# A two-layer encoder trunk in fp32r: another mixer, with scores on row halves, two heads' probabilities side by side, another order of products, and an output projection fed with normalised blocks

## The chip, the core and the metric

The kernel runs on one core of one Trainium2 chip. That core has TensorE (PE, with weight loads shown apart as PEld), VectorE (DVE), ScalarE (ACT), GpSimd (POOL) and SyncE (SP), which here only issues DMAs. The metric is device time in microseconds of one execution, lower is better. The chip has a multiplier array of 128 rows; a matmul multiplies a stationary tile (loaded first) with a moving tile and adds into one of eight PSUM banks of 128 x 512 floats.

## The reference, cut to what matters

The trunk has two layers on x of 256 tokens x 1024 channels. Each layer is a half-step SwiGLU, the mixer, a second half-step SwiGLU, and a gated per-layer input; a final norm follows. Only the mixer is changed:

```python
u = rmsnorm(x, g_mix[i]) @ w_in[i]
q, k, v, hy = jnp.split(u, [NA_WIDTH, 2 * NA_WIDTH, 3 * NA_WIDTH], axis=-1)
hs = (B, L, NA_HEADS, NA_HEAD_DIM)          # 8 heads of 64
y_na = neighbourhood_attention(q.reshape(hs), k.reshape(hs), v.reshape(hs), na_rpb[i])
hy = short_conv(hy, w_sc[i], b_sc[i])        # width 3 over the tokens
x0, x1, hv = jnp.split(hy, 3, axis=-1)
filt = implicit_filter(...)                  # independent of x
y_hy = x0 * long_conv(hv * x1, filt, hy_bias[i])
y = jnp.concatenate([_rms(y_na), _rms(y_hy)], axis=-1) * g_out[i]
x = x + y @ w_out[i]
```

Attention is a masked softmax over the 256 tokens for each of the 8 heads; `_rms` divides each token's 512 channels by their root mean square, once for the attention half (NA) and once for the convolution half (HY).

## The kernel before

Channels lie on the 128 partitions and the 256 tokens along the free axis, so x is eight tiles of 128 x 256. Every product is made with operands split into a high and a low fp32r part: `mm3` (lines 169 to 173) issues high x high, high x low and low x high. Weights stream from HBM in pieces of 16 tiles; ACT casts the high part (line 285) and DVE or, for every third half piece in the mixer, POOL subtracts to get the low part (line 288). Six half pieces are held ready.

The order of the program comes from generators ("fibers"). The main program issues PE work; after every three units of it (a unit is an `mm3` on 256 columns) `tick` advances every live fiber by one step, the newest first. When PE work needs a fiber's result, `finish` runs `tick` until that fiber is done, without any PE work in between. PE and ACT run in the order in which the program recorded their instructions; DVE, POOL and SP stand in the order that a scheduler gave them when the program was built. Each queue is served strictly in its order.

The mixer (lines 662 to 1000) first makes the values of all heads, then follows the table `ORDER` (line 58), whose letters mean: `q` j, queries and keys of head pair j; `g` j, the two convolution inputs that are multiplied to u[j] (POOL, line 854); `x`, the outer gate x0; `s` j, the scores of pair j, followed by a softmax fiber (DVE bias and maximum, ACT exponential, DVE reciprocal, ACT rescale, line 779); `t` j, transposes of the probabilities (line 786) and their split in high and low; `p` j, probabilities times values; `u`, transposes of u; `f` 0 and 1, the forward transform of u, followed by `spectral` fibers (DVE products with the filter's spectrum, lines 900 and 901, POOL sums, line 906, ACT cast, line 910, DVE low part, line 912) that leave `yf`; `i` 0 to 3, the backward transform, which needs all four `yf`; `a` 0 to 7, the output projection's half for NA.

Three choices of the old code matter below. In `QK.go` the queries of the two heads of a pair are written into a zeroed 128-row tile, one head's rows at a time, so that each head's scores are a full-height matmul with half of its rows zero. In `attend` each head's values stand in zero-padded columns, so both heads add into one 128 x 256 result. In `head_norm` the blocks are scaled by the gain only; the projection starts on them at once, and the result of each projection is multiplied by the token's 1/rms afterwards (`add`, lines 942 and 943). The 1/rms comes from class `Rstd`: two small PE matmuls on the summed squares (line 418), a chain of small DVE instructions (lines 426 to 435) with two on ACT (line 436), and two PE matmuls with `ones` that spread it over the partitions (lines 442 and 443); `rest` counts the ticks between these steps.

Of the kernel before, what the change touches and what calls it, by code (L numbers as in the profile page):

```python
# [18 lines left out]
P = 128  # L19
T = 256  # L20
# [37 lines left out]
ORDER = "g0 q0 g1 s0 q1 g2 t0 s1 g3 q2 t1 p0 u0 q3 f0 s2 f1 p1 s3 t2 x0 x1 t3 i0 p2 p3 i1 i2 i3 a0 a1 a2 a3 a4 a5 a6 a7"  # L58
MIXER = [(t[0], int(t[1])) for t in ORDER.split()]

# [20 lines left out]
def hybrid_trunk(ctx: ExitStack, tc: tile.TileContext, w, xT, pT, rpb, small, wf, zT, dft, idft, decay, out):  # L81
# [322 lines left out]
    class Rstd:  # L404
# [6 lines left out]
        def go(self, parts, n, behind, at):  # L411
# [32 lines left out]
            S.copy(self.dst, ps)  # L444
# [222 lines left out]
    def mixer(i):  # L667
# [25 lines left out]
        vh = [[t2(F32R, "vh") for _ in range(2)] for _ in range(2)]  # L693
        vl = [[t2(F32R, "vl") for _ in range(2)] for _ in range(2)]

        def values():
            for tt in range(2):
                for pp in range(2):
                    G.memset(f(vh[tt][pp]), 0.0)
                    G.memset(f(vl[tt][pp]), 0.0)  # L700
            yield from rs.wait()
            for tt in range(2):
                vf = t2()
                V.tensor_scalar(vf, vps[tt], rs.r[:, tt : tt + 1], None, op0=ALU.mult)
                yield
                for pp in range(2):
                    src = vf[:, pp * 256 : (pp + 1) * 256].rearrange("p (a b c) -> p a b c", a=2, b=2)
                    hv, lv = v2(vh[tt][pp]), v2(vl[tt][pp])
                    for par in range(2):
                        cs = slice(par * 192, par * 192 + 64)  # L710
                        S.copy(hv[:, :, cs], src[:, :, par])
                    yield
                    for par in range(2):
                        cs = slice(par * 192, par * 192 + 64)
                        V.tensor_sub(lv[:, :, cs], src[:, :, par], f(hv[:, :, cs]))

        class QK:


            def __init__(self, b):  # L720
                self.kh, self.kl = t1(F32R), t1(F32R)
                self.qh, self.ql = t2(F32R), t2(F32R)
                self.fb = spawn(self.go(b))

            def go(self, b):
                G.memset(f(self.qh), 0.0)
                G.memset(f(self.ql), 0.0)
# [5 lines left out]
                where = [  # L733
                    (slice(64 * par, 64 * par + 64), slice(T * par, T * par + T)) for par in range(2)
                ]
                S.copy(self.kh, q[:, T:])
                for r, c in where:
                    S.copy(self.qh[r, c], q[r, :T])
                yield
                V.tensor_sub(self.kl, q[:, T:], f(self.kh))  # L740
                for r, c in where:
                    V.tensor_sub(self.ql[r, c], q[r, :T], f(self.qh[r, c]))

        class Head:
# [7 lines left out]
            def scores(self, st):  # L752
                st.fb.finish()
                b = bank()
                for tt in range(2):
                    qs = slice(T * self.par + tt * P, T * self.par + (tt + 1) * P)
                    mm3(b[:, tt * T : (tt + 1) * T], st.qh[:, qs], st.ql[:, qs], st.kh, st.kl, True, True)
                self.e = t2()
                self.fb = spawn(self.softmax(b), True)
# [21 lines left out]
            def turn(self):  # L781
                self.fb.finish()
                b = bank()
                for kt in range(2):
                    for tt in range(2):
                        PE.transpose(
                            b[:, kt * T + tt * P : kt * T + (tt + 1) * P],
                            self.e[:, tt * T + kt * P : tt * T + (kt + 1) * P],
# [471 lines left out]
```

## Time and profile before

| what | value |
|---|---|
| median of three runs | 1099.89 us (1099.7 to 1102.32) |
| the profiled execution | 1098.94 us, of which the span is 1097.2 us |
| mean granted TensorE clock | 0.994 |
| busy share of the span | PE 97%, DVE 83%, ACT 59%, POOL 24% |
| mixer of layer 1, of layer 2 | about 206.5 to 331 us, about 750 to 866 us of the span |

A row of the timeline gives the start in us, the busy time in us, engine, line, operation, written tile and read tiles, shape and how often; in brackets stands the idle time of that engine just before and the instruction that ended it. Instructions of one engine overlap in their records (a 256-column matmul lasts 0.28 us and the next starts 0.12 us later), so what one costs in a full queue is the distance from start to start.

### The profile page before, as it was taken

To read this page: it belongs to the slowest core of one execution; us is meant where nothing else is said; L and a number is where in the kernel's file an instruction comes from. 1 tells how busy PE (TensorE), PEld (TensorE's weight loads), DVE (VectorE), ACT (ScalarE), POOL (GpSimd) and SP (SyncE) were. 2 spreads that over 40 slices of the span, in tenths; PEclk is the share of its full clock that TensorE was granted. 3 is DMA by queue.
4 is the path that set the end of the run, shared out by engine and by line. 5 is a ranking of instruction groups with operands and counts; after the bars stand their busy time and mean duration, and the time that the engine had idled before them with its cause. 6 is when DMAs were issued, how large, how long until landed. Compare 5 with 4: busy or idle time off the path is not lost.

```text
span 1097.2 us, 18014 instructions
## 1 busy us (share of the span) xinstructions
PE 1066.1 (97%) x6716; PEld 964.1 (88%) x6716; DVE 912.0 (83%) x1552; ACT 649.2 (59%) x1182; POOL 266.1 (24%) x270
## 2 busy tenths in 40 slices
PE   7989999999998999999999999999999999999995
PEld 6878888899997888888988888889989888888895
DVE  4999987798999988856789999787899998886565
ACT  7566565367746766554666665544856476665444
POOL 3211120534363211100112113025442721110101
PEclk9989999999999999999999999999999999999998
DMA  8556545554425555555465654554622465554621
GB/s 318 199 202 227 192 163 183 177 180 163 154 78 201 196 192 193 188 192 177 169 211 184 231 192 158 188 177 168 194 78 90 151 220 202 192 192 159 208 94 39
DMA packets 32983, 194.07 MB, mean 177 GB/s; under 512 B 3584, under 2 KB 6528, under 8 KB 10880
## 3 DMA queue, kind: packets, MB, share of 16 engines
q1 hardware_dynamic: 32896, 192.92, 51.4%
q8 instruction: 53, 0.87, 0.3%
q14 instruction: 34, 0.28, 0.1%
HBM read 191.86 MB, written 1.05 MB: 176 GB/s over the span
## 4 chain that ended last, share of the span: by engine, by line
PE 79%; DVE 13%; ACT 4%; issue 3%; DMA 0%; POOL 0%; SPq 0%; DVEq 0%; ACTq 0%; POOLq 0%
PE ps L191 41%; PE ps L200 21%; PE ps L171 5%; PE ps L172 5%; PE ps L170 5%; DVE wl L288 3%; ACT wh L285 1%; DVE s L839 1%; DVE rt L399 1%; DVE x L943 1%; DVE s L942 1%; ACT t L779 1%; DVE xg L370 1%; ACT t L772 0%; DVE y L808 0%
## 5 line engine op out<-in xcount | busy, mean ns | idle before, releaser
L288 DVE TENSOR_TENSOR wl<-raw,wh 128x1024 fp32r<-128x1024 f32 (+1 forms) x328 | 405.3, 1258 | 103.2 <-PE ps L200 61.3
L285 ACT CAST wh<-raw 128x1024 fp32r<-128x1024 f32 (+1 forms) x350 | 362.4, 1042 | 157.0 <-PE ps L191 86.1
L191 PE MATMUL ps<-xg,wh 128*128 128x512 f32 x1408 | 347.3, 396 | 12.9 <-DVE xg L1091 6.7
L191 PEld LDWEIGHTS ps<-xg,wh 128*128 128x128 f32 x1408 | 260.0, 191 | 64.7 <-DVE xg L370 8.1
L200 PEld LDWEIGHTS ps<-xg,wl 128*128 128x128 f32 x1408 | 182.1, 191 | 7.7
L200 PE MATMUL ps<-xg,wl 128*128 128x256 f32 x1408 | 184.2, 283 | 0.0
L191 PE MATMUL ps<-act,wh 128*128 128x512 f32 x704 | 173.0, 391 | 0.0
L490 POOL TENSOR_TENSOR gu<-gu,rb 128x256 f32<-128x256 f32 x88 | 69.6, 796 | 394.4 <-DVE gu L208 326.3
L191 PEld LDWEIGHTS ps<-act,wh 128*128 128x128 f32 x704 | 128.3, 189 | 23.9
L356 POOL TENSOR_TENSOR acc<-acc,q 128x256 f32<-128x256 f32 x62 | 55.9, 902 | 295.0 <-ACT q L353 293.8
L170 PE MATMUL ps<-xg,wh 128*128 128x256 f32 x448 | 127.5, 285 | 0.0
L171 PE MATMUL ps<-xg,wh 128*128 128x256 f32 x448 | 126.7, 283 | 0.0
L172 PE MATMUL ps<-xg,wl 128*128 128x256 f32 x448 | 126.7, 283 | 0.0
L200 PEld LDWEIGHTS ps<-act,wl 128*128 128x128 f32 x704 | 92.9, 191 | 5.1
L200 PE MATMUL ps<-act,wl 128*128 128x256 f32 x704 | 94.4, 282 | 0.0
L171 PEld LDWEIGHTS ps<-xg,wh 128*128 128x128 f32 x448 | 85.9, 192 | 0.1
L170 PEld LDWEIGHTS ps<-xg,wh 128*128 128x128 f32 x448 | 85.9, 192 | 0.1
L172 PEld LDWEIGHTS ps<-xg,wl 128*128 128x128 f32 x448 | 85.9, 192 | 0.0
L205 ACT COPY gu<-ps 128x256 f32<-128x256 f32 x176 | 56.2, 374 | 33.1 <-PE ps L200 32.7
L288 POOL TENSOR_TENSOR wl<-raw,wh 128x1024 fp32r<-128x1024 f32 x22 | 56.1, 2550 | 64.0 <-ACT wh L285 51.2
L208 DVE TENSOR_TENSOR gu<-gu,ps 128x256 f32<-128x256 f32 x176 | 66.3, 413 | 0.0
L368 ACT ACTIVATE xg<-x,sm 128x256 fp32r<-128x256 f32 x56 | 28.2, 508 | 59.3 <-DVE x L527 39.9
(196 smaller groups left out, 1386.9 us busy)
## 6 DMA issues: line engine op xcount, KB each, us to landing
raw<-in_w SPq DMA_DIRECT2D x172, 1024.0 KB, 5.0
bias<-in_rpb SPq DMA_DIRECT2D x16, 256.0 KB, 2.9
raw<-in_w SPq DMA_DIRECT2D x4, 256.0 KB, 4.4
x<-in_xT SPq DMA_DIRECT2D x8, 128.0 KB, 5.0
raw<-in_w SPq DMA_DIRECT2D x2, 512.0 KB, 5.5
t<-in_wf SPq DMA_DIRECT2D x4, 256.0 KB, 5.6
dec<-in_decay SPq DMA_DIRECT2D x4, 256.0 KB, 6.3
out<-o SPq DMA_DIRECT2D x4, 256.0 KB, 2.5
```

Source lines behind the costliest of these rows:

```text
L170: PE.matmul(o, lh, rh, start=start, stop=False)
L171: PE.matmul(o, lh, rl, start=False, stop=False)
L172: PE.matmul(o, ll, rh, start=False, stop=stop)
L191: PE.matmul(b, lh, r, start=start, stop=False)
L200: PE.matmul(o, ll, rh, start=False, stop=stop)
L205: S.copy(dst, b[:, T:])
L208: V.tensor_add(dst, dst, b[:, :T])
L285: S.copy(h[:, a : a + k], src)
L288: e.tensor_sub(l[:, a : a + k], src, f(h[:, a : a + k]))
L356: G.tensor_add(self.ac, self.ac, q)
L368: S.activation(hl[:, :T], x[c], AF.Copy, scale=g)
L490: G.tensor_mul(u, u, rb)
```

## The change

The diff touches the mixer only (all line numbers after it are one or more off: `mm3` is lines 170 to 174 there):

- `QK`: queries and keys stay together in one 128 x 512 tile, split by one ACT cast and one DVE subtraction; the zeroed tiles are gone. `scores`: each head uses its own 64 rows of the array, and the matmuls of the two heads alternate, into two banks.
- `turn`: the two heads' transposed probabilities of one half of the keys share a bank. `attend`: one matmul on 512 columns serves both heads; two ACT copies take each head's 64 rows out of the bank, and the square follows on a later tick. Values need no padding.
- `Rstd` with `dst` True leaves 1/rms in its PSUM bank. `normed` and the new `head_norm` wait for it, multiply each block by gain and 1/rms (DVE), cast (ACT) and subtract (DVE); only then is a block ready for the projection. `add` is one DVE addition from PSUM to x. The NA half of the projection is issued after the four backward products, the HY half after it.
- `ORDER` is new; "g1+s0" puts the scores between the two products of g1. The weights are laid out in HBM in the new order.

```diff
-ORDER = "g0 q0 g1 s0 q1 g2 t0 s1 g3 q2 t1 p0 u0 q3 f0 s2 f1 p1 s3 t2 x0 x1 t3 i0 p2 p3 i1 i2 i3 a0 a1 a2 a3 a4 a5 a6 a7"
+ORDER = "q0 g0 q1 g1+s0 q2 g2+s1 t0 q3 p0 g3+s2 t1 x0+s3 u0 p1 t2 f0 t3 f1 p2 p3 x1 i0 i1 i2 i3"
...
-            S.copy(self.dst, ps)
+            if self.dst is True:
+                self.dst = ps
+            else:
+                S.copy(self.dst, ps)
...
+                S.activation(vh[tt], vps[tt], AF.Copy, scale=r)
+                yield
+                V.scalar_tensor_tensor(vl[tt], vps[tt], r, f(vh[tt]), op0=ALU.mult, op1=ALU.subtract)
...
+                S.copy(self.h, q)
+                yield
+                V.tensor_sub(self.l, q, f(self.h))
...
-        def head_norm(src, sq, ch, hl):
-
-            g = col(i, C_OUT + ch)
-            S.activation(hl[:, :T], src, AF.Copy, scale=g)
-            sq.add(src)
-            yield
-            V.scalar_tensor_tensor(hl[:, T:], src, g, f(hl[:, :T]), op0=ALU.mult, op1=ALU.subtract)
+        def head_norm(ch, st, y, hl):
+
+            yield from st.wait()
+            h, l = hl[:, :T], hl[:, T:]
+            V.scalar_tensor_tensor(y, y, col(i, C_OUT + ch), st.dst, op0=ALU.mult, op1=ALU.mult)
+            yield
+            S.copy(h, y)
+            V.tensor_sub(l, y, f(h))
...
+            b = bank()
+            for kt, (h, l, fb) in enumerate(ps):
+                fb.finish()
+                vs = slice(128 * pair, 128 * pair + 128)
+                mm3(b, vh[kt][:, vs], vl[kt][:, vs], h, l, kt == 0, kt == 1)
+            y = ys[0][pair]
+
+            def go():
+                for par in range(2):
+                    r = slice(64 * par, 64 * par + 64)
+                    S.copy(y[r], b[r, T * par : T * par + T])
+                yield
+                nsq.add(y)
+                yield
...
+            st.fb.finish()
+            banks = [bank(), bank()]
+            for tt in range(2):
+                qs = slice(tt * P, (tt + 1) * P)
+                for n, (a, b) in enumerate(((st.h, st.h), (st.h, st.l), (st.l, st.h))):
+                    for par, o in enumerate(banks):
+                        r = slice(64 * par, 64 * par + 64)
+                        PE.matmul(o[:, tt * T : (tt + 1) * T], a[r, qs], b[r, T:], start=n == 0, stop=n == 2)
+                paced(2)
...
-        def add(c, ps, st, e):
-            yield from rest(EV)
-            yield from st.wait()
-            t = t1()
-            V.tensor_mul(t, ps, st.dst)
-            e.tensor_add(x[c], x[c], t)
...
+        def normed(parts, sq, at, spread, ch):
+            st = Rstd(True, sq.parts, HY, [fb for _, fb in parts], at, spread)
+            made = []
+            for c, (y, _) in enumerate(parts):
+                hl = t2(F32R, "yn")
+                made.append((hl, spawn(head_norm(ch + c, st, y, hl))))
+            return made
...
+        hy = normed(yhy, hsq, STAT_HY, SPREAD_HY, 4)
+        wo = Tiles()
+
+        def add(c, o):
+            yield from rest(EV)
+            V.tensor_add(x[c], x[c], o)
+
+        added = [spawn(add(c, project(wo, na))) for c in range(KD)]
```

What this does to the queues is shown at three places of layer 1.

Place 1, ACT, from the exponentials of the fourth head pair's softmax to the rescaling that its transposes wait for. Before (t641 and t643 are the two heads' probabilities, wh a weight cast, t469 and t471 casts for the backward transform):

```order
L772 ACTIVATE t641_3235,su660_3300<-t650_3262,mx651_3264 128x256 x2
L772 ACTIVATE t643_3243,su661_3303<-t652_3266,mx653_3268 128x256 x2
L285 CAST wh663_3322<-raw579_2943 128x1024
L910 CAST t469_2358<-t638_3228 128x512
L910 CAST t471_2360<-t628_3189 128x512
L779 ACTIVATE t641_3235<-t641_3235,ri665_3330 128x256 x2
L779 ACTIVATE t643_3243<-t643_3243,ri666_3332 128x256 x2
```

Now (t615 and t616 are that pair's probabilities; the casts of L212 are the transposed u at the top and the third pair's transposed probabilities below, y463 an attention block, x0623 and x0624 the outer gate):

```order
L212 CAST t629_3189<-ps628_3184 128x512
L212 CAST t626_3182<-ps625_3177 128x512
L749 ACTIVATE t615_3130,su632_3199<-t619_3153,mx620_3155 128x256 x2
L749 ACTIVATE t616_3131,su633_3202<-t621_3157,mx622_3159 128x256 x2
L790 COPY y463_2352<-ps631_3191 64x256 x2
L212 CAST t635_3213<-ps634_3208 128x512
L212 CAST t638_3220<-ps637_3215 128x512
L354 ACTIVATE q642_3234<-y463_2352 128x256
L805 ACTIVATE x0623_3175<-t641_3225,sm_84 128x256
L805 ACTIVATE x0624_3176<-t641_3225,sm_84 128x256
L756 ACTIVATE t615_3130<-t615_3130,ri643_3239 128x256 x2
L756 ACTIVATE t616_3131<-t616_3131,ri644_3241 128x256 x2
```

Before, three casts stood between the exponentials and the rescaling. Now the two casts of the transposed u stand ahead of the exponentials, and seven instructions of other steps, two of which read an attention product of PE and two a transpose of PE, stand between them and the rescaling (line 756).

Place 2, DVE, around the low part of the last spectral block (`yf[3]`, tile t474 in both programs), which the first backward product reads. Before:

```order
L830 TENSOR_TENSOR t672_3387<-ps657_3278,rb_104 128x512
L839 SCALAR_TENSOR_TENSOR x0667_3363<-t672_3387,sm_84,x0667_3363 128x255
L840 SCALAR_TENSOR_TENSOR x0667_3363<-t672_3387,sm_84,x0667_3363 128x255
L839 SCALAR_TENSOR_TENSOR x0668_3364<-t672_3387,sm_84,x0668_3364 128x255
L912 TENSOR_TENSOR t474_2363<-t648_3256,t473_2362 128x512
L840 SCALAR_TENSOR_TENSOR x0668_3364<-t672_3387,sm_84,x0668_3364 128x255
L288 TENSOR_TENSOR wl675_3399<-raw604_3079,wh674_3398 128x1024
L830 TENSOR_TENSOR t687_3470<-ps669_3365,rb_104 128x512
L797 TENSOR_TENSOR t680_3442<-ps678_3436,t679_3441 128x512
L797 TENSOR_TENSOR t683_3449<-ps681_3443,t682_3448 128x512
L948 SCALAR_TENSOR_TENSOR s688_3483<-u485_2441,sm_84,ps684_3450 128x256
```

Now, behind the DVE chain of NA's `Rstd` (L765 is the multiplication by 1/rms, which reads PSUM bank ps694 that the `ones` matmuls write; L768 the low part of a normalised block):

```order
L908 TENSOR_TENSOR t472_2361<-t657_3304,t471_2360 128x512
L811 SCALAR_TENSOR_TENSOR x0691_3437<-t693_3440,sm_84,x0691_3437 128x255
L811 SCALAR_TENSOR_TENSOR x0692_3438<-t693_3440,sm_84,x0692_3438 128x255
L812 SCALAR_TENSOR_TENSOR x0691_3437<-t693_3440,sm_84,x0691_3437 128x255
L812 SCALAR_TENSOR_TENSOR x0692_3438<-t693_3440,sm_84,x0692_3438 128x255
L765 SCALAR_TENSOR_TENSOR y464_2353<-y464_2353,sm_84,ps694_3450 128x256
L765 SCALAR_TENSOR_TENSOR y463_2352<-y463_2352,sm_84,ps694_3450 128x256 x2
L768 TENSOR_TENSOR yn665_3324<-y464_2353,yn665_3324 128x256
L768 TENSOR_TENSOR yn664_3323<-y464_2353,yn664_3323 128x256
L768 TENSOR_TENSOR yn663_3322<-y463_2352,yn663_3322 128x256
L768 TENSOR_TENSOR yn662_3321<-y463_2352,yn662_3321 128x256
L908 TENSOR_TENSOR t474_2363<-t671_3350,t473_2362 128x512
```

Before, t474 stood among the outer gate's additions, ahead of NA's `Rstd`. Now it stands behind that `Rstd`, the outer gate's four additions, NA's multiplications by 1/rms (the first of them is the row ahead of these) and NA's four low parts. In layer 2 it stands ahead of the four low parts.

Place 3, DVE, behind the DVE chain of HY's `Rstd`. Before (L942 and L943 add projections to x, s774.. are their products):

```order
L435 TENSOR_SCALAR s757_3774<-ident_99,rh755_3770 128x128 x2
L942 TENSOR_TENSOR s760_3791<-ps739_3719,rna475_2364 128x256
L942 TENSOR_TENSOR s761_3804<-ps740_3732,rna475_2364 128x256
L942 TENSOR_TENSOR s767_3831<-ps759_3787,rna475_2364 128x256
L288 TENSOR_TENSOR wl742_3734<-raw673_3390,wh741_3733 128x1024
L288 TENSOR_TENSOR wl772_3846<-raw724_3637,wh771_3845 128x1024
L942 TENSOR_TENSOR s776_3876<-ps766_3824,rhy476_2365 128x256
L942 TENSOR_TENSOR s777_3879<-ps762_3807,rhy476_2365 128x256
L943 TENSOR_TENSOR x1_86<-x1_86,s776_3876 128x256
```

Now (yn700 to yn703 are the four HY blocks that the second half of the projection reads):

```order
L436 TENSOR_SCALAR s736_3682<-ident_99,rh734_3678 128x128 x2
L765 SCALAR_TENSOR_TENSOR y466_2355<-y466_2355,sm_84,ps743_3719 128x256 x2
L289 TENSOR_TENSOR wl722_3642<-raw673_3355,wh721_3641 128x1024
L765 SCALAR_TENSOR_TENSOR y465_2354<-y465_2354,sm_84,ps743_3719 128x256 x2
L768 TENSOR_TENSOR yn703_3532<-y466_2355,yn703_3532 128x256
L768 TENSOR_TENSOR yn702_3531<-y466_2355,yn702_3531 128x256
L768 TENSOR_TENSOR yn701_3530<-y465_2354,yn701_3530 128x256
L768 TENSOR_TENSOR yn700_3529<-y465_2354,yn700_3529 128x256
L992 TENSOR_TENSOR x0_85<-x0_85,ps739_3711 128x256
```

Before, PE needed nothing of these rows for its projections; they only took results out of PSUM. Now the HY projections wait for the last of the four L768, with a weight's low part between the multiplications.

More of the change, by code (lines that the diff above doesn't have):

```diff
@@ L750, in __init__, with scored @@
                 nc.sync.dma_start(self.bias, rpb[i, 2 * pair + par])
[L752 to L757, printed above, removed]
+            def scored(self, b):
                 self.e = t2()
@@ L779, in softmax @@
                     S.activation(e[:, cs], e[:, cs], AF.Copy, scale=ri[:, tt : tt + 1])
[L781 to L788, printed above, removed]
-                            ident,
-                        )
-                self.h, self.l = t2(F32R), t2(F32R)
-                self.fb = spawn(self.parts(b), True)
@@ L810, in attend @@
[L810 to L823 removed]
+        yna, yhy = [], []
```

135 lines of the change are left out of this document (51 added, 84 removed).

## The prediction

> **What bounds the kernel now.** I read the page first, then the mixer's stretches of the span, then the order of starts inside them.
>
> ```profile
> PE 1066.1 (97%) x6716; PEld 964.1 (88%) x6716; DVE 912.0 (83%) x1552; ACT 649.2 (59%) x1182; POOL 266.1 (24%) x270
> PE 79%; DVE 13%; ACT 4%; issue 3%; DMA 0%; POOL 0%; SPq 0%; DVEq 0%; ACTq 0%; POOLq 0%
> ```
>
> PE is busy for 97% of the span and carries 79% of the chain that ended last, so the time is the number of PE slots plus PE's pauses. The windows of the mixer (columns: window, length, then busy time and instructions of PE, PEld, DVE, ACT, POOL, the granted clock) show the pauses; the first two rows are layer 1 with the start of the SwiGLU behind it, the other two layer 2:
>
> ```profile
> 206.50:331.00 124.50, 123.09 (x947) 118.31 (x946) 109.92 (x210) 76.34 (x157) 58.54 (x51) 1.00 0.44 145
> 331.00:348.00 17.00, 13.69 (x75) 11.38 (x75) 17.00 (x23) 13.04 (x26) 9.32 (x8) 1.00 0.58 198
> 750.00:866.00 116.00, 113.26 (x902) 109.97 (x900) 105.31 (x203) 72.25 (x151) 49.62 (x42) 1.00 0.40 133
> 866.00:881.00 15.00, 12.77 (x68) 10.66 (x69) 15.00 (x22) 11.04 (x21) 10.81 (x8) 1.00 0.52 179
> ```
>
> PE idles 1.41 + 3.31 us in layer 1 and 2.74 + 2.23 us in layer 2, 9.7 us in all. In the rows behind the mixer DVE is busy for every microsecond while PE waits: there DVE is the bound. DVE does the old projection's multiplications and additions at the same time as POOL does its share, and its additions take 1.0 us where a subtraction of the same 256 columns (below) takes 0.34:
>
> ```profile
> L943 DVE TENSOR_TENSOR x<-x,s 128x256 f32<-128x256 f32 x16 | 15.7, 1012 | 0.0
> L943 POOL TENSOR_TENSOR x<-x,s 128x256 f32<-128x256 f32 x16 | 15.3, 986 | 2.4 <-DVE s L942 2.4
> ```
>
> **The change, part by part.** First what PE saves. Start-to-start distances give a slot:
>
> ```profile
> 213.13 0.39 PE L172 MATMUL ps<-wh,xg 128*128 128x512 f32 x1
> 213.36 0.39 PE L170 MATMUL ps<-wh,xg 128*128 128x512 f32 x1
> ...
> 264.18 0.28 PE L172 MATMUL ps<-xg,wl 128*128 128x256 f32 x1
> 264.30 1.04 PE L786 MATMUL ps<-ident,t 128*128 128x128 f32 x8
> 265.09 0.36 PE L170 MATMUL ps<-t,vh 128*128 128x256 f32 x1
> 265.29 0.28 PE L171 MATMUL ps<-t,vh 128*128 128x256 f32 x1
> 265.41 0.28 PE L172 MATMUL ps<-t,vl 128*128 128x256 f32 x1
> ```
>
> A slot on 512 columns is 0.23 us, on 256 columns 0.12 us, eight transposes 0.79 us.
>
> - Scores: 12 matmuls a pair, 12 × 0.12 = 1.44 us. On row halves, if two run side by side, 0.72 us. No row here shows matmuls on halves, so the gain over eight pairs lies between 0 and 5.8 us. The change of shape has a neighbour: the first matmul behind the transposes holds its slot 0.20 us instead of 0.12, so in and out of eight groups costs at most 16 × 0.08 = 1.3 us. I take the whole 5.8, since the two matmuls touch disjoint rows of the array and different banks. The Trainium skill, "TensorEngine Tiling (Array Packing)", Key Properties, says that different tiles load and multiply in parallel, and also that a change of the tiling mode drains TensorE; no run here shows either yet, and by its first rule the gain is the same 5.8 us.
> - Products with values: 12 × 0.12 = 1.44 becomes 6 × 0.23 = 1.38 us, over eight pairs −0.5 us.
> - The additions to x become one DVE instruction from PSUM instead of a multiplication and an addition, and POOL leaves. Of the 9.7 us of visible pauses I leave 1.0: −8.7 us.
>
> The zeroed tiles' memsets and the smaller subtractions lie on DVE and POOL beside busy PE; they are worth nothing beyond that.
>
> Now what PE newly waits for. The order of each queue is fixed, so I follow layer 1 by hand from the start of x0's first product (T = 0). PE alone would end the transposes of u at 7.2, the fourth pair's transposes at 14.1, reach NA's statistics matmuls at 23.0 and end the first backward product at 26.2. The durations, other engines:
>
> ```profile
> 287.07 0.51 ACT L772 ACTIVATE t<-t,mx 128x256 f32<-128x256 f32 x1
> 287.57 0.50 ACT L772 ACTIVATE t<-t,mx 128x256 f32<-128x256 f32 x1
> ...
> 291.03 1.72 ACT L779 ACTIVATE t<-t,ri 128x256 f32<-128x256 f32 x4
> 292.64 1.05 ACT L285 CAST wh<-raw 128x1024 fp32r<-128x1024 f32 x1
> 293.58 1.11 ACT L833 ACTIVATE x<-t,sm 128x256 f32<-128x256 f32 x2
> 294.57 0.63 ACT L910 CAST t<-t 128x512 fp32r<-128x512 f32 x1
> ...
> 307.06 0.40 ACT L353 ACTIVATE q<-s 128x256 f32<-128x256 f32 x1
> ```
> ```profile
> 303.89 0.74 POOL L356 TENSOR_TENSOR nacc<-nacc,q 128x256 f32<-128x256 f32 x1 [1.09 <-ACT q L353]
> 314.50 2.58 POOL L288 TENSOR_TENSOR wl<-raw,wh 128x1024 fp32r<-128x1024 f32 x1
> ```
> ```profile
> 276.65 0.69 DVE L900 TENSOR_TENSOR t<-ps,spec 128x512 f32<-128x512 f32 x1
> 277.26 0.68 DVE L901 TENSOR_TENSOR t<-ps,spec 128x512 f32<-128x512 f32 x1
> ...
> 310.38 0.87 DVE L948 SCALAR_TENSOR_TENSOR s<-u,sm,ps 128x256 f32<-128x256 f32 x2
> 311.16 0.76 DVE L950 TENSOR_TENSOR s<-s,x 128x256 f32<-128x256 f32 x2
> 311.83 1.23 DVE L288 TENSOR_TENSOR wl<-raw,wh 128x1024 fp32r<-128x1024 f32 x1
> 312.98 0.96 DVE L808 SCALAR_TENSOR_TENSOR y<-s,sm,y 128x256 fp32r<-128x256 f32 x1
> ...
> 318.42 0.14 DVE L426 TENSOR_SCALAR v<-ps 128x2 f32<-128x2 f32 x1
> ...
> 322.27 1.08 DVE L942 TENSOR_TENSOR s<-ps,rna 128x256 f32<-128x256 f32 x3
> ```
>
> From start to start: an exponential 0.50 us, a rescaling 0.40 (1.61 for four), a convolution step 0.50, a 512-column cast 0.50, a weight cast 0.95, a square 0.40; on POOL a sum of squares 0.74, a weight's low part 2.5; on DVE a spectrum product or 512-column low part 0.61, a gated product 0.39, a 256-column subtraction 0.34, a weight's low part 1.15, and the whole chain of `Rstd` 318.42 to 322.27, 3.85 us.
>
> 1. u[3] is a POOL product that stands behind DVE's convolution additions, and these behind ACT's exponentials of pair 2. I find it ready at 8.0, and the transposes end at 8.5: +1.2 us in layer 1. In layer 2 u[3] stands earlier: 0.
> 2. ACT from 8.7, place 1: 2 casts, 4 exponentials, 2 copies, 2 casts, a square, 2 convolution steps, 4 rescalings, about 7.6 us by these rows. The fourth pair's transposes end at 16.8 instead of 14.1 + 1.2: +1.5, and the copies of u's transposes that PE meets ahead of them give another 1.1: +2.6.
> 3. PE reaches the statistics at 23.0 + 3.8 = 26.8. Pairs 2 and 3 end at 22.3; two copies, a weight cast and a square on ACT, then on POOL the low part ahead of them and the last two sums (2.5 + 2 × 0.74) make about 28.6: +1.8.
> 4. `ones` stands nine matmuls (1.1 us) behind the statistics: PE would be there at 29.8, the chain of 3.85 us with its two ACT steps ends at 32.9: +3.1. Before, 47 matmuls covered it; `finish` in the backward product runs the ticks off without PE work.
> 5. The last matmul of the first backward product needs the low part of yf[3], place 2. Behind the diagonals DVE still does 2 × 0.61 for the gate and yf[1], the first normalised block 0.4, yf[2] 0.61, four convolution additions and three blocks 7 × 0.4, four low parts 4 × 0.34, then 0.61: 32.9 + 7.0 = 39.9. PE would be there at 34.6: +5.3. In layer 2 the four low parts come behind it: +3.9.
>
> Middle: 14.0 us in layer 1, 0 + 2.6 + 1.8 + 3.1 + 3.9 = 11.4 us in layer 2.
>
> 6. Place 3, HY. Between its statistics and `ones` lie 18 matmuls, 2.2 us; the chain, with two additions to x of 0.34 between its steps and 0.3 for ACT, takes 4.8: +2.5. Behind `ones` the HY half of the projection starts on the first block, which DVE makes last of four: 4 × 0.39, a weight's low part 1.15, 4 × 0.34: +4.1. That is 6.6 us a layer, 13.2 us.
>
> **Sum**, in the profiled execution's 1098.94 us: −5.8 − 0.5 − 8.7 + 14.0 + 11.4 + 13.2 = +23.6, 1122.5; the median lies 0.95 above that execution, so 1123 us. Lower bound: items 1 to 3 are hidden, leaving 3.1 + 5.3 and 3.1 + 3.9, and HY 11.0 (each of its four waits 0.55 shorter): 1098.9 − 15.0 + 15.4 + 11.0 = 1110; with the DVE instructions a quarter shorter than these rows, another 6 less: 1104. Upper: halves in series +5.8 and 1.3: 1130; or the clock, next.
>
> **Rivals.** The clock. One pause inside the span was over 3 us:
>
> ```profile
> 70.00 0.58 PE L560 MATMUL ps<-s,t 128*128 128x256 f32 x1 [3.58 <-DVE s L544]
> ```
> ```profile
> 65.00:70.00 5.00, 1.42 (x11) 0.98 (x10) 4.13 (x11) 3.45 (x8) 0.79 (x1) 0.93 0.77 262
> 70.00:75.00 5.00, 5.00 (x13) 4.03 (x14) 5.00 (x8) 3.91 (x9) 0.74 (x1) 0.50 0.51 156
> 75.00:80.00 5.00, 5.00 (x29) 4.38 (x28) 5.00 (x11) 2.81 (x6) 0.74 (x1) 0.89 0.73 267
> ```
>
> (Columns as in the windows above.) Behind it the granted clock was 0.50 for 5 us and part of both neighbours, 6.8 us at half speed, so 3.4 us of work lost. My HY pause of 4.1 us is just longer than 3.58; two of them cost 6.8 (1130 us), and with the middles up to four, 13.6 (1137 us). The pause is split from the one before it by two matmuls, and a seventh off my DVE sum brings it under the row's length, so it is not in the likeliest case. The Trainium skill, "TensorE: Matmul & The Clock Gate", Part 1, has the clock drop to half after about one idle window of 3.4 us and return after as long a busy stretch; the row of 3.58 us agrees. Chance 0.22.
>
> Halves in series: no gain from the scores, 1123 + 7 = 1130. Against it, nothing but that no row shows it. Chance 0.12.
>
> Milder middle: items 1 to 3 hidden, 1104 to 1113. For it: in the windows ACT has slack of a third. Chance 0.14.
>
> Only the tail: every middle wait is covered because DVE, with less to do, reaches yf[3] ahead of PE; then 1098.9 − 15.0 + 13.2 + 0.95 = 1098, no change. Chance 0.06.
>
> The other side: the `Rstd` chains and their blocks are covered throughout. HY's first block would have to be ready within the 2.2 us of 18 matmuls, or the scheduler's order hides it; all of the 15.0 us is kept: 1085 us. It decides once the new waits of a layer are under 7.5 us, and speaks for it that DVE before had 14.6 and 10.7 us free in the first rows of windows. Against it: the chain alone is 3.85 us, serial whoever is idle. Chance 0.10.
>
> **How the numbers follow.** Forecast (1114 to 1127): 0.36; with the rivals 0.22 + 0.12 + 0.14 + 0.06 + 0.10. A measurement here tells about 0.3%, 3.3 us, from no change. Faster 0.10, same 0.06, slower 0.84. The range 1104 to 1138 leaves out the same, the faster case and a little above: under 2 in 10.
>
> **What would show it.** In the changed kernel's waits of PE: the fourth pair's transposes on ACT's rescaling; statistics on POOL's nacc; `ones` on DVE's or ACT's diagonals, some 3 us; the backward product on yf[3]'s low part, the longest in the middle; the projection on a normalised block's low part or cast, some 4 us, twice. Scores' starts 0.06 us apart on average if the halves run side by side, 0.12 if not. A granted clock under 1.00 behind a pause proves the clock rival. Wrong is the whole if PE's pauses in the mixer stay under 15 us for both layers together; then my hand-followed queue order overstates the waits.

## The result and the profile after

| | before | changed |
|---|---|---|
| median | 1100.01 us (1099.7 to 1102.32, 4 runs) | 1136.38 us (1135.26 to 1136.77, 4 runs) |
| span of the profiled execution | 1097.2 us | 1134.7 us |
| mean granted TensorE clock | 0.994 | 0.970 |

The changed kernel is slower: ratio 1.0327, 95% interval 1.0311 to 1.0342. The first rows of the page after (busy time, share of the span and instructions of each engine; then the chain that ended last, by engine):

```profile
PE 1079.8 (95%) x6676; PEld 971.6 (86%) x6676; DVE 895.9 (79%) x1520; ACT 650.5 (57%) x1166; POOL 236.9 (21%) x220
PE 86%; DVE 6%; ACT 4%; DMA 2%; POOL 1%; issue 1%; SPq 0%; DVEq 0%; POOLq 0%; ACTq 0%
```

PE issues 40 instructions fewer, DVE, ACT and POOL have less to do than before or as much, and PE is busy 13.7 us longer. Longer with less work: that is mostly the clock, as the windows below show. What PE waited for in the changed kernel (total, times, longest):

```profile
PE ps L443 <- DVE s L436: 8.2, 4, 3.1
PE ps L192 <- DVE xg L1090: 6.6, 1, 6.6
PE ps L171 <- ACT yn L767: 6.6, 2, 3.3
PE ps L173 <- DVE t L908: 5.6, 4, 3.0
PE ps L419 <- POOL nacc L357: 5.6, 2, 3.2
PE ps L564 <- DVE s L548: 3.6, 1, 3.6
PE ps L172 <- DVE yn L768: 3.4, 2, 1.7
PE ps L846 <- ACT t L756: 3.0, 2, 1.5
PE ps L1064 <- ACT s L1055: 2.7, 2, 1.5
PE ps L878 <- POOL u L826: 0.7, 1, 0.7
```

The rows of L1090, L564 and L1064 stand in the program's start and end and were there before. The other seven are new, 33.1 us, all in the two mixers. Their places in layer 1, from the timeline of PE:

```profile
286.08 2.52 PE L846 MATMUL ps<-ident,t 128*128 128x128 f32 x8 [1.54 <-ACT t L756]
...
303.01 0.61 PE L419 MATMUL ps<-onesf,nacc 128*128 128x1 f32 x4 [3.17 <-POOL nacc L357]
...
307.13 0.58 PE L443 MATMUL ps<-s,ones 128*128 128x256 f32 x1 [2.11 <-DVE s L436]
...
309.69 0.58 PE L173 MATMUL ps<-idft_h,t 128*128 128x256 f32 x1 [0.41 <-DVE t L908]
...
314.38 0.58 PE L173 MATMUL ps<-idft_h,t 128*128 128x256 f32 x1 [3.05 <-DVE t L908]
...
334.75 0.38 PE L443 MATMUL ps<-s,ones 128*128 128x256 f32 x1 [1.67 <-DVE s L436]
...
338.98 0.58 PE L171 MATMUL ps<-yn,wh 128*128 128x256 f32 x1 [3.32 <-ACT yn L767]
341.26 0.58 PE L172 MATMUL ps<-yn,wh 128*128 128x256 f32 x1 [1.70 <-DVE yn L768]
```

They come in the order that the prediction lists: the fourth pair's transposes, NA's statistics, its `ones`, yf[3]'s low part, HY's `ones`, HY's first block. The granted clock over the same place (windows, columns as in the prediction):

```profile
285.00:290.00 5.00, 3.71 (x12) 2.85 (x13) 3.53 (x8) 3.40 (x8) 0.46 (x1) 0.73 0.00 0
...
300.00:305.00 5.00, 1.99 (x13) 1.71 (x13) 3.58 (x9) 0.00 (x0) 2.96 (x2) 0.94 0.54 177
305.00:310.00 5.00, 2.48 (x9) 2.03 (x9) 4.55 (x16) 3.29 (x8) 0.00 (x0) 0.50 0.08 33
310.00:315.00 5.00, 1.95 (x9) 1.66 (x9) 4.33 (x12) 1.43 (x4) 0.00 (x0) 0.50 0.00 0
315.00:320.00 5.00, 5.00 (x32) 5.00 (x32) 2.50 (x6) 1.77 (x3) 0.74 (x1) 0.70 0.00 0
...
335.00:340.00 5.00, 1.24 (x3) 0.57 (x2) 4.30 (x6) 3.32 (x7) 2.93 (x1) 0.51 0.00 0
340.00:345.00 5.00, 3.74 (x17) 3.74 (x18) 1.62 (x5) 0.00 (x0) 0.00 (x0) 0.50 0.62 210
```

Each layer has three stretches at half clock: 287.32 to 290.73, 304.38 to 318.04 and 335.10 to 345.34 us in layer 1. Layer 2 shows the same picture 550 us later. The six last 54.6 us, and PE is busy for 36.4 us of them.

Of the waits of the kernel before, these are gone:

```profile
PE ps L191 <- DVE xg L370: 6.2, 6, 1.9
...
PE ps L786 <- ACT t L779: 1.2, 1, 1.2
PE ps L170 <- ACT t L738: 0.8, 2, 0.6
PE ps L171 <- DVE s L740: 0.7, 2, 0.3
PE ps L882 <- POOL u L854: 0.2, 1, 0.2
```

The span grew by 37.5 us, and the two traces account for it: new waits +33.1, old ones −9.1; scores −2.7 (below) and products with values −0.5 (1.44 us a pair before and 1.39 now, in a full queue); and as PE's busy time rose by 13.7 us although these took 3.2 us from it, 16.9 us more were put on it. The sum is +37.7. The 16.9 is what remains and was not measured by itself, but the slow clock accounts for its size: half of the 36.4 us of busy time at half clock is 18.2.

The scores' share comes from PE's timeline of the first group on row halves:

```profile
238.15 0.28 PE L173 MATMUL ps<-xg,wl 128*128 128x256 f32 x1
238.36 0.39 PE L865 MATMUL ps<-t 64*128 64x256 f32 x2
238.58 0.40 PE L865 MATMUL ps<-t,t 64*128 64x256 f32 x4
238.82 0.28 PE L865 MATMUL ps<-t 64*128 64x256 f32 x2
238.94 0.40 PE L865 MATMUL ps<-t,t 64*128 64x256 f32 x4
239.27 0.39 PE L171 MATMUL ps<-xg,wh 128*128 128x256 f32 x1
239.49 0.28 PE L172 MATMUL ps<-xg,wh 128*128 128x256 f32 x1
```

The halves do run side by side: the twelve matmuls take 0.91 us (238.36 to 239.27) where twelve slots of 0.12 are 1.44. But that is 0.19 more than half, and the slots just ahead of the group and just behind it, 0.21 and 0.22 us, are 0.1 us longer each. What is won is 0.34 us a pair, and the other seven groups show the same within 0.01: 2.7 us in all.

### The profile page after: what moved, and what is told of

It reads as the page before. It is cut to its first block, busy times and chain, and to the rows that moved or that the text cites. A ratio compares the mean times of both kernels' runs of the same rounds, so it can differ in the third digit from the quotient of the medians.

```text
span 1134.7 us, 17781 instructions
## 1 busy us (share of the span) xinstructions
PE 1079.8 (95%) x6676; PEld 971.6 (86%) x6676; DVE 895.9 (79%) x1520; ACT 650.5 (57%) x1166; POOL 236.9 (21%) x220
## 4 chain that ended last, share of the span: by engine, by line
PE 86%; DVE 6%; ACT 4%; DMA 2%; POOL 1%; issue 1%; SPq 0%; DVEq 0%; POOLq 0%; ACTq 0%
PE ps L192 40%; PE ps L201 21%; PE ps L171 8%; PE ps L173 8%; PE ps L172 8%; DVE wl L289 1%; DMA raw<-in_w 1%; ACT wh L286 1%; DVE rt L400 1%; DVE yn L768 1%; PE ps L419 1%; PE ps L865 1%; ACT t L749 1%; ACT t L212 1%; DMA bias<-in_rpb 1%
## 5 line engine op out<-in xcount | busy, mean ns | idle before, releaser
L289 DVE TENSOR_TENSOR wl<-raw,wh 128x1024 fp32r<-128x1024 f32 (+1 forms) x328 | 410.7, 1274 | 113.0 <-PE ps L201 62.7
L494 POOL TENSOR_TENSOR gu<-gu,rb 128x256 f32<-128x256 f32 x88 | 72.2, 826 | 399.6 <-DVE gu L209 337.2
```

The source lines that it names most:

```text
L289: e.tensor_sub(l[:, a : a + k], src, f(h[:, a : a + k]))
L494: G.tensor_mul(u, u, rb)
```

## The experiments

All ratios are to runs of the kernel before on the same chip, with 95% intervals. The theory: the arithmetic is innocent; PE waits because the new order and the normalisation ahead of the projection put too little independent PE work behind the start of a serial chain on DVE, ACT and POOL, and the clock falls in and behind these pauses. The rival: the new forms (row halves, side-by-side probabilities, reads of 1/rms from PSUM) cost time themselves.

### Scores alone

```diff
 # the kernel before, with QK and scores of the change
-mm3(b[:, ...], st.qh[:, qs], st.ql[:, qs], st.kh, st.kl, True, True)
+PE.matmul(o[:, tt * T : (tt + 1) * T], a[r, qs], b[r, T:], start=n == 0, stop=n == 2)
```

> The kernel before with one part of the change: queries and keys in one tile, the two heads' scores on row halves; order, products with values, projection as before. In the trace after, a group of 12 took 1.34 us from the last matmul ahead of it to the second behind it, against 14 x 0.12 = 1.68 at full height. If the halves run side by side with that price at each end: 8 x 0.34 = 2.7 us less than before, about 1097.3 us. If they gain all (the prediction's term): 5.8 less, 1094.2. If the change of shape costs what it saves, or the two new matmul forms are part of the loss: 1100 or more.

1097.81 us, ratio 0.9989 (0.9979 to 1.0). The measured gain is 1.8 us against the runs of before, by the interval 0 to 2.3. It excludes a cost and the 5.8 us of the prediction, and it falls a little short of 2.7. In its profile PE's busy time is 3.6 us shorter than before, but PE's waits are 2.6 us longer in sum.

### The order undone

```diff
-ORDER = "q0 g0 q1 g1+s0 q2 g2+s1 t0 q3 p0 g3+s2 t1 x0+s3 u0 p1 t2 f0 t3 f1 p2 p3 x1 i0 i1 i2 i3"
+ORDER = "g0 q0 g1 s0 q1 g2 t0 s1 g3 q2 t1 p0 u0 q3 f0 s2 f1 p1 s3 t2 x0 x1 t3 i0 p2 p3 i1 i2 i3"
```

> The changed kernel with the order of before (projection still on normalised blocks, behind all backward products). If the order makes the middle waits (NA statistics, ones, yf[3], the fourth pair's transposes: about 9.9 us of waits a layer and 3.5 of slow clock), most of them go, but NA's 1/rms then has only three backward products, 4.3 us, ahead of the first projection, so some 3 to 5 us come back there: 1112 to 1122 us. HY's waits of 6.7 us a layer stay. If the order has no part in it: 1133 or more.

1111.29 us, ratio 1.0114 (1.0101 to 1.0128): 25.1 us less than the changed kernel, just under the expected stretch. The waits at NA's statistics and the backward product are all but gone. In layer 1 PE's pauses over 1 us are now these:

```profile
308.36 0.56 PE L443 MATMUL ps<-s,ones 128*128 128x256 f32 x1 [3.71 <-DVE s L436]
313.12 0.58 PE L171 MATMUL ps<-yn,wh 128*128 128x256 f32 x1 [3.85 <-ACT yn L767]
...
315.25 0.42 PE L419 MATMUL ps<-onesf,hacc 128*128 128x1 f32 x2
...
325.67 0.28 PE L443 MATMUL ps<-s,ones 128*128 128x256 f32 x1
```

That is a surprise in its form: HY's waits were expected to stay. The pause of 7.6 us, at `ones` and at the first projection, is now NA's, and HY waits for nothing. HY's statistics stand at 315.25, among the first matmuls of the projection, and its `ones`, 10.4 us later, finds the chain done. So HY's pause in the changed kernel is no property of HY. The same chain makes a pause or none by the PE work between its statistics and its first reader.

### The normalisation undone

```diff
 # the changed kernel; both halves scaled behind the projection, squares and POOL's additions as before (shortened)
-V.scalar_tensor_tensor(y, y, col(i, C_OUT + ch), st.dst, op0=ALU.mult, op1=ALU.mult)
+S.activation(hl[:, :T], src, AF.Copy, scale=g)          # gain only
...
-V.tensor_add(x[c], x[c], o)
+V.tensor_mul(t, ps, st.dst)
+e.tensor_add(x[c], x[c], t)
```

> The changed kernel with the old tail: blocks scaled by the gain only, 1/rms multiplied in after the projection, squares and additions to x as before; the new order, scores and products with values stay. If HY's pause comes from the normalisation ahead of the projection, 6.7 us of waits and 2.1 of slow clock a layer go, 17.5 us; of the middle, the yf[3] wait shrinks by 2 to 3 us a layer since the four blocks no longer stand ahead of it; the old pauses behind the mixer come back, about 5.5 us in all: 1118 to 1124 us. If the HY pause has another cause: 1133 or more.

1114.6 us, ratio 1.0145 (1.013 to 1.016): 21.8 us less, more than expected. Besides HY's pause the statistics' waits fell from 5.6 to 1.3 us and yf[3]'s from 5.6 to 0.6. But NA's `ones` waits longer, 9.3 us instead of 5.2:

```profile
PE ps L443 <- DVE s L436: 9.3, 2, 5.0
PE ps L173 <- DVE t L907: 0.6, 2, 0.3
```

The gain at the statistics is thus a wait that moved: they came earlier, but the first instruction of the chain stood behind a weight's low part on DVE (299.09 to 301.39 us in layer 1). The gain at yf[3] is real: with the four blocks off the DVE queue the reader of its low part starts 4.3 us behind the start of `ones` in layer 1 and not 7.25.

### Order and normalisation undone together

```diff
 # the heads' arithmetic of the change; order and tail of before
+ORDER = "g0 q0 g1 s0 q1 g2 t0 s1 g3 q2 t1 p0 u0 q3 f0 s2 f1 p1 s3 t2 x0 x1 t3 i0 p2 p3 i1 i2 i3"
 # and the tail of the run above
```

> The new heads' arithmetic alone (scores on row halves, the two heads' probabilities side by side, unpadded values), with the order of before and the tail of before (1/rms after the projection). If the loss is wholly in order and normalisation: the run with scores alone plus 6 instead of 12 slots in the products, 0.06 us a pair, that is 1096.5 to 1098. If the side-by-side form (one wide product, two copies on half the rows) has a cost of its own: 1100 or more.

1098.15 us, ratio 0.9982 (0.9973 to 0.9992). This closes a square: changed 1136.4, order undone 1111.3, normalisation undone 1114.6, both undone 1098.2 (the runs of before on these chips stand at 1099.6 to 1100.0). Either alone wins 25.1 and 21.8 us, both 38.2, less than their sum, since several pauses need both: HY's waits go with either. The rival falls for the scores, products and values: with the new ones all in place the kernel is level with the one before, or 0.2% faster. Its ratio is the lowest of all, though by less than the 0.3% that the prediction takes for noise, and with scores alone it is not apart from it. The reads of 1/rms from PSUM are not in this kernel. In the changed one they last 0.48 us each (L765), as the product with another PSUM operand does (L934), so no price of their own shows.

### The pauses filled

```diff
+def keep(b, n):                       # results that nobody reads; shortened
+    for _ in range(n):
+        PE.matmul(b[:, T:], ones, idft_h[:, 0], start=True, stop=True)
...
+keep(pc, 20)   # ahead of NA's statistics; 16 ahead of its ones
+keep(nst.pc, 28)   # ahead of yf[3]'s first reader
+keep(hst.pc, 34)   # ahead of HY's projection; 12 ahead of its ones
```

> The changed kernel with matmuls that no result uses put into the pauses (20 ahead of NA's statistics, 16 ahead of its ones, 28 ahead of the last matmul of the first backward product, 12 ahead of HY's ones, 34 ahead of HY's projection, of 0.12 us each at full clock), so that PE is not idle there; nothing waited for is changed. The slow clock covered 27.3 us a layer in the trace after; PE worked 8.4 of those at double length. If all that counts: 16.7 us less, 1120. If the part of it that lies beside the waits is free and only what is behind the last wait counts (1.8 and 2.1 us a layer, and 1.7 behind the fourth pair's transposes, which has no filler and stays): 7.8 less, 1128.6. If the clock costs nothing: 1136.

1126.65 us, ratio 1.0251 (1.0237 to 1.0265): 9.7 us less with 220 matmuls more. The mean clock rose from 0.970 to 0.989. That the slow clock costs time is thus shown. What filling won is less than the 16.9 us put on PE's busy time. Two reasons fit: the stretch behind the fourth pair's transposes was left unfilled and stayed (287.76 to 291.17 us), and slow matmuls ahead of a wait cost nothing, since the wait ends when it ends. The second is what the expectation of 7.8 us rested on; it was not tested by itself. Most of the 27 us that the filled kernel still has over the one before is the waits, now filled.

### HY's normalisation alone undone

```diff
-hy = normed(yhy, hsq, STAT_HY, SPREAD_HY, 4)
+hy = Rstd(t1(s="rhy"), hsq.parts, HY, [fb for _, fb in yhy], STAT_HY, SPREAD_HY)
...
+V.tensor_mul(t, o, hy.dst)
 V.tensor_add(x[c], x[c], t)
```

> The changed kernel with HY's half alone scaled behind the projection; NA, heads and order as changed. HY's own share is then measured: 6.7 us of waits and 2.1 us of slow clock a layer, 17.5 us less, and 1 to 4 us of pauses behind the mixer back: 1119 to 1123 us. If HY's pause only moves to the additions behind it: 1128 or more.

1115.43 us, ratio 1.0156 (1.0137 to 1.0176): 21.0 us less, beyond the expected 17.5 less 1 to 4. The pause behind the mixer came back with 2.0 us, HY's 13.1 us of waits are gone, and with them the slow stretch behind them. The stretch at half clock behind the fourth pair's transposes was missing too in this profile, in both layers, though the pause of 1.5 us ahead of them was there as before; that was not foreseen, and it makes part of the surplus. In this order NA's normalisation then costs little more: with both halves' normalisation undone the kernel is at 1114.6.

### Other orders: can the chains be covered?

Three kernels keep the normalisation and seek cover for it:

```diff
-ORDER = "... t1 x0+s3 u0 p1 t2 f0 t3 f1 p2 p3 x1 i0 i1 i2 i3"
+ORDER = "... t1 s3 p1 t2 u0 x0 t3 p2 p3 f0 f1 x1 i0 i1 i2 i3"      # both halves normalised; and NA alone
+ORDER = "... t1 s3 p1 t2 x0+u0 t3 p2 f0 p3 f1 x1 i0 i1 i2 i3"      # NA alone, second form
```

> The changed kernel, both halves normalised ahead of the projection, with another order: the third and fourth pairs' products ahead of the forward transform, so that NA's statistics have 6 wide and 30 narrow matmuls (5 us) before ones and all four backward products before the first projection; HY's statistics and ones asked for earlier (45 matmuls, 5.4 us, between them instead of 18). If only missing cover makes the pauses: the middle waits all but go (yf[3] may keep 1 to 2 us a layer), HY's ones is covered, and only the four blocks behind it, 4 to 5 us a layer, stay with their slow clock: 1098 to 1104. If the normalised blocks cost as such: 1110 or more.

> As the run that covers both, but HY's half is scaled behind the projection as in the kernel before, so nothing waits for HY's 1/rms but the additions. If cover decides: no pause of over 2 us in the mixer, clock as in the kernel before; of the 15.0 us that the change can win (9.7 of old pauses less 1.0 kept, 2.7 of scores, 0.5 of products) 8 to 12 are seen: 1087 to 1093. If the order cannot cover NA's chain either: 1100 or more.

> As the run that covers NA, with the fourth pair's products between the two forward transforms: NA's statistics come 18 matmuls later, its ones still stands 36 matmuls (4.3 us) behind them, at the head of the backward product. If the distance statistics to ones against a chain of 4.2 us decides, a wait of under 1 us at ones and 1 to 3 us at yf[3], which now stands behind the four blocks again: 2 to 6 us above the run that covers NA. If only the total cover up to the first projection counts: the same within 1.5 us.

(In these, NA's `rest` count ahead of the statistics is also set lower, and in the first HY's two.) They took 1129.25 us (ratio 1.027, 1.0255 to 1.0285), 1118.67 (1.0173, 1.0158 to 1.0188) and 1120.72 (1.0188, 1.0171 to 1.0205). The first two missed by 25 us and more. The third is 2.1 us above the second, as one of its cases has it, but the two intervals overlap, and its `ones` waits up to 2.7 us where under 1 was expected. In the second, PE's waits read

```profile
PE ps L173 <- DVE t L908: 7.2, 4, 2.9
...
PE ps L846 <- ACT t L756: 4.7, 2, 2.7
...
PE ps L443 <- DVE s L436: 4.5, 2, 2.3
```

The wait at the statistics is gone, but each move took cover from another chain: the fourth pair's softmax now stands too near its transposes (a wait of 1.5 us in the changed kernel, 2.7 here), and between the forward transform and the backward product stands x1 alone, so yf is late. The run with both normalised differs from it only in HY (its normalisation and `rest` counts) and is 10.6 us slower, which is HY's pause and clock once more.

A fourth kernel moves only the third and fourth pairs' products in the order of before, and a fifth is the same with both halves scaled behind the projection:

```diff
-ORDER = "... s3 t2 x0 x1 t3 i0 p2 p3 i1 i2 i3"
+ORDER = "... s3 t2 x0 t3 p2 p3 x1 i0 i1 i2 i3"
```

> The order of before with one move: the third and fourth pairs' products stand ahead of the second outer product x1 instead of behind the first backward product. NA's half is normalised ahead of the projection, HY's scaled behind it; the heads' arithmetic is new. In the two runs that moved these products ahead of the forward transforms, the new pauses stood at the fourth pair's transposes (its softmax too near) and at yf (the forward transform too near the backward one); here both stand as far apart as before to within 3 us, and NA's statistics have 38 matmuls (4.6 us) ahead of ones and 70 ahead of the first projection. If distance is all: pauses in the mixer of 6 us or less over both layers, 1090 to 1096 us. If normalised blocks cannot be covered in this mixer: 1103 or more, with the pause at the first projection.

> As the run with NA covered, but both halves scaled behind the projection, so that the two differ in NA's normalisation alone. The pauses behind the mixer stay as in the run of the heads' arithmetic alone (6.9 us), the moved products cost or win under 2 us: 1096 to 1100. If normalising NA early is worth its lighter additions, this run is 3 to 6 us above the run with NA covered; if not, it is level with it or below.

1108.01 us (1.0078, 1.006 to 1.0095) and 1104.2 us (1.0043, 1.0028 to 1.0059). The times hoped for, 1090 to 1096 and 1096 to 1100, were both missed. In the first the waits are

```profile
PE ps L419 <- POOL nacc L357: 5.9, 2, 3.1
PE ps L172 <- DVE yn L768: 3.7, 2, 2.0
```

`ones` is nearly covered, as 38 matmuls against the chain of 4.2 us should have it, but the statistics again stand too near the last sum of squares on POOL, and the low part of a block comes up to 2.0 us late for the first projection. Normalising NA early wins nothing over scaling it behind: the pair, which differs in two of NA's `rest` counts beside the normalisation, stands 3.8 us apart the other way. And the move of the products itself costs some 6 us against the heads' arithmetic in the old order, where less than 2 were expected; 3.9 us of it is the same wait at the statistics. No order that I tried makes the normalised form faster than the kernel before. That none exists is not shown.

### POOL's part

```diff
-ON_POOL = 3
+ON_POOL = 0        # in the mixer, every weight's low part on DVE
```

> The changed kernel with one thing moved: in the mixer DVE makes every weight's low part, POOL none (11 a layer go from POOL at 2.5 us to DVE at 1.2). If POOL's low part ahead of the last sum of squares makes the wait of NA's statistics, and the one that ran beside HY's four low parts made these 2.8 us instead of 1.4: of 2.8 us of waits a layer at the statistics some 2 go, at the HY blocks 1.4, 6 to 8 in all: 1128 to 1131 us. If DVE, with 13 us more a layer, comes late in the tails where these waits end: 1134 or more.

1134.01 us, ratio 1.0306 (1.0282 to 1.033): at the edge of the second case, and its interval overlaps that of the changed kernel. Both mechanisms are there. POOL in the changed kernel, ahead of the last sum of squares, and DVE at the same time:

```profile
298.48 2.81 POOL L289 TENSOR_TENSOR wl<-raw,wh 128x1024 fp32r<-128x1024 f32 x1
301.25 1.70 POOL L357 TENSOR_TENSOR nacc<-nacc,q 128x256 f32<-128x256 f32 x1
```
```profile
299.14 3.23 DVE L289 TENSOR_TENSOR wl<-raw,wh 128x1024 fp32r<-128x1024 f32 x1
```

The two engines hold each other up here: DVE's low part takes 3.23 us instead of 1.2 and ends 1.1 us after POOL's, and POOL's sum takes 1.70 us instead of 0.74 (as it does without POOL's low part, again beside one on DVE). Without POOL's low part the waits at the statistics fell from 5.6 to 0.4 us. And HY's four low parts on DVE, in the changed kernel beside a low part on POOL (336.98 to 339.91), with the first of the four alone, then without one on POOL:

```profile
338.41 2.80 DVE L768 TENSOR_TENSOR yn<-y,yn 128x256 fp32r<-128x256 f32 x4
338.41 1.79 DVE L768 TENSOR_TENSOR yn<-y,yn 128x256 fp32r<-128x256 f32 x1
```
```profile
338.43 1.42 DVE L768 TENSOR_TENSOR yn<-y,yn 128x256 fp32r<-128x256 f32 x4
```

The first alone makes the difference; it ends 0.3 us after POOL's low part. But the gain is given back at the next wait:

```profile
PE ps L443 <- DVE s L436: 9.6, 4, 3.3
PE ps L171 <- ACT yn L767: 8.9, 2, 4.5
```

`ones` waits 1.4 us longer and HY's first block 2.3 us, since DVE now makes two weights' low parts (2.35 us) in the middle of the blocks. 5.2 us won at the statistics and 2.8 at the low part become 2.4 us between the medians, which is not clear of the noise.

## Why the prediction was right, and where not

The direction and the range held: 1136.4 us in 1104 to 1138. The likeliest case, 1123, missed by 13 us; what came was the rival with the clock (1130, or 1137 with four events), to which I gave 0.22. The range holds because it reached up to that rival.

| step | predicted | measured |
|---|---|---|
| scores | −5.8 us | −2.7 |
| products with values | −0.5 | −0.5 by their slots |
| old pauses | −8.7 | −9.1 |
| 1, u[3] | +1.2 | +0.7 |
| 2, fourth pair's transposes | +5.2 | +3.0 (4.8 with the pace of the transposes, below) |
| 3, NA's statistics | +3.6 | +5.6 |
| 4, NA's `ones` | +6.2 | +5.2 |
| 5, yf[3] | +9.2 | +5.6 |
| 6, HY's `ones` and first block | +13.2 | +13.1 |
| clock | 0 in the likeliest case | +16.9 in PE's busy time, as remainder; 9.7 of the time won by filling |

(Both layers. The waits of `ones` are split by their place: 2.11 and 3.05 for NA, 1.67 and 1.38 for HY.)

**The waits.** Their six places and causes were right, their sum 38.6 against 33.1. Step 5 is the largest difference, and its reason shows in the timeline. The reckoning for DVE, 7.0 us from `ones` to yf[3]'s low part, was right (7.25 in layer 1). But PE took 4.2 us to come there from `ones` instead of 1.7, because it ran at half clock and waited 0.41 us on the way. Step 2 was nearly right: its row counts the wait ahead of the first transposes only, and the next three started 0.40 us apart, at the pace of the rescalings, where a full queue has 0.10. That is another 0.9 us a layer, which the accounts above have in PE's busy time. Step 3 was low by 2.0 us over both layers: POOL still had a spectrum sum (297.23, 1.29 us in the timeline) ahead of the weight's low part. Only one sum of squares was left behind that, but it took 1.70 us instead of 0.74, beside DVE's low part. In step 6 the sum is right by luck: HY's `ones` waited 3.05 us instead of 5.0, and the first block 10.0 instead of 8.2, the latter because the first of the four low parts took 1.79 us beside POOL.

```profile
297.23 1.29 POOL L902 TENSOR_TENSOR t<-t,t 128x512 f32<-128x512 f32 x1
```

The causes are tested, not only read: the middle waits go with the old order, all but NA's `ones`; HY's go with the old tail, and with the old order too; the statistics' go with POOL's low part.

**What failed** is the step "it is not in the likeliest case", on the clock. I had one row, a pause of 3.58 us with half clock behind it, forecast pauses of 4.1 to 5.3 us, and left the clock out because the 4.1 us could come out a little shorter; the 5.3 us of step 5 was longer than the row even so. That compared single pauses, where the trace should have been read by the stretch: over 300 to 315 us PE was busy 6.4 of 15 us, in pieces. A longest pause of 3.3 us was enough. The rival's price was right in size, 13.6 us for four events against 9.7 us won by filling and 16.9 in PE's busy time, but not its form: there are three stretches a layer, and the longest has 13.7 us at half clock and not 6.8.

**The scores** failed by half: that two halves run side by side was right, and the 1.3 us for changes of shape, which the upper bound had, belonged in the sum. 0.19 us inside each group and 0.19 at its ends, eight times, take 3.1 of the 5.8 us. The 1.3 us came from the row behind the transposes, 0.08 us twice a group, and were too little as well. The Trainium skill's rule on the drain when the tiling mode changes ("TensorEngine Tiling (Array Packing)", Key Properties) agrees with the 0.21 us ahead of the first half-height matmul, where a slot is 0.12. But a slot of 0.20 us also stands behind full-height transposes in the kernel before (265.09), so the runs do not show that this rule is the cause.

With scores at −2.7 and the clock at the 9.7 us that filling wins, the sum of the prediction would be 1122.5 + 3.1 + 9.7 = 1135.3 in the profiled execution, 1136.3 as a median. That this is so near the 1136.4 is partly luck: the waits' sum was 5.5 us too high, and the clock's part is 9.7 us by filling but 16.9 us by the busy time.

**The other rivals.** A tail only, milder middles and full cover: none came, and nothing supports them. The halves in series: excluded by the starts.

## What to carry to other kernels

A serial chain (sum, statistics, reciprocal root, spread, scale, split) costs nothing while there is independent PE work between its first input and its first reader, and its full length otherwise: count both distances, in slots and in microseconds, for every reader that a change moves closer. Scaling after a product instead of before it is such a distance bought with a few extra instructions on another engine. When forecast pauses leave PE less than half busy over some 3.4 us (the step in which this case's clock moved, below), put the slow clock into the sum and not among the rivals, even if no single pause is that long. And an order that brings one chain's cover must be checked for the chain that it takes it from.

## What the runs showed of the hardware that was not expected

- The clock also fell behind short pauses. In both layers of the changed kernel a pause of 1.5 us ahead of eight transposes (286.08) was followed by 3.4 us at half clock (mean 0.73 and 0.93 in two windows of 5 us in layer 1). In the kernel before, the stretches behind the mixers had pauses up to 1.9 us and kept 1.00.
- The stretches at half clock in the mixers of all profiles last 3.4, 6.8, 10.2 or 13.7 us, whole multiples of 3.41 us. I divided each of the fourteen profiles, from 60 to 1060 us, into the steps of 3.41 us that its stretches mark. All 43 steps at full clock in which PE was busy for at most 0.45 of the time were followed by half clock, and none above 0.62 was. Between the two both happened: 283.90 to 287.31 in the changed kernel was busy for 1.66 us and followed by half clock, 338.90 to 342.31 in the kernel before for 1.52 us and was not. What decides there stays open.
- Beside a POOL subtraction of 128x1024 the first of four 256-column subtractions on DVE took 1.79 us, to 0.3 us behind POOL's end, and the four 2.80; without it they took 1.42. DVE's two products with a PSUM operand just ahead of them ran beside the same POOL instruction at their usual 0.47 us.
- A group of twelve matmuls on 64 rows each has a fixed cost of some 0.4 us beside its twelve half slots: the matmuls of a pair start 0.003 to 0.004 us apart, a pair takes 0.115 us, and the slots at the group's two ends and the first and last pair are each some 0.1 us longer.
